# Modulation vectors of a two-layer backbone: which engine makes the first shift, and when the late vectors are made

## The chip, the cores and the metric

One core of one Trainium2 chip. The metric is the device time of one launch in microseconds (us), as the median of several runs.

## What is computed

One step of a two-layer backbone over 1024 latent tokens and 128 context tokens, width 1024, all in 32-bit floats. Each layer modulates its normalised input with vectors that depend only on the two conditions (`c` for the latent tokens, `c_ctx` for the context tokens):

```
m = silu(cond) @ w_ada + b_ada            # cond: 2 x 1024, w_ada: 1024 x 6144, per layer
sh1, sc1, g1, sh2, sc2, g2 = split(m, 6)  # parts 0 to 5, 1024 numbers each
h = rms_norm(x) * (1 + sc1) + sh1         # then layer 0: pooling + latent attention; layer 1: neighbourhood attention
x = x + g1 * mixer(h)
h = rms_norm(x) * (1 + sc2) + sh2
x = x + g2 * (square(relu(h @ w1)) @ w2)  # MLP, hidden width 4096
```

The change concerns only `m`: 2 layers x 6 parts x 2 conditions.

## The kernel before, in words

Activations lie transposed, channels on the 128 partitions, tokens along the free axis (1152 of them). Each 32-bit product is made from two rounded halves in three matmuls (`mm3`, L331). Tiles come from 36 slots of SBUF (`Slots`, L51): a new tile takes the slot that was freed longest ago. All DMAs are issued by SyncE (SP), one queue in order. The order of instructions on each engine is not the program's order: a list scheduler with a timeline of its own orders them when the kernel is built, taking on each engine the earliest program step that is ready in its timeline. What the hardware then does is in order on each engine.

A modulation vector is made in one of two ways.
- **On TensorE**, `ada_mat(part)` (L217): eight loads of 512 KB (`wadan`, each in its own slot), per load two matmuls of 512 columns with the 2-column condition as the stationary side (each appears as two instructions in the trace), then eight small transposes (`ps_at`) and the bias. Parts 0 and 1 of layer 0 are made so, one after the other, scale first, at the very start.
- **On VectorE**, `ada_gen(layer, fs)` (L192): per block `f` of 128 outputs one load of 512 KB into one of two tiles (`wada`, or a tile of the weight ring `wr` with `ring`), and two multiply-and-sum instructions (L201, `trash<-wada,silu`), one for each condition, each followed by a read of the accumulator. They need `silu`, the conditions broadcast to all partitions: two tiles of 512 KB that `silu_load` (L183) reads from a small DRAM tensor, which is stored once from a transposed copy (L520 to L524). A part is 8 blocks, 16 such instructions. After block 7 of a part, `ada_bias` finishes it.

`background(n)` (L236) takes n steps (n L201 instructions) from a list of such generators. It is called inside other loops, so that the instructions come between those of the loop.

Where the parts are made before: layer 0, parts 0 and 1 on TensorE at the start; parts 2 and 3 in the background of the input projection (L617 to L637, `NBG` = 4 steps for each tile); parts 4 and 5 by `ada_late` (L1114), run in a block after the attention of layer 0 and ahead of its output projection (`out_group`, L880). Layer 1: parts 0 and 1 in the MLP of layer 0 (`tail0(-1)`, steps in `second_tile`, L459); parts 2 to 5 in the input projection of layer 1 (L1197 to L1214, `QBG` = 2).

The attention of layer 0 (L1091 to L1110) runs head by head. `attend_units(h)` (L1057): for each of two halves nine key tiles, per tile three score matmuls (`ps_st`), an exponential on ScalarE, and the product with the values (`ps_pv`). Woven into it for heads 0 to 5 is `max_units(h+2)` (L1028), which finds the row maxima of a head two ahead: 24 matmuls (`ps_m`, three PSUM buffers) and for each a VectorE reduction (L1037). At the end of each pair of heads `recip_pair` (L1043) divides. At the start of each head the next heads' tensors are loaded, ten larger loads. TensorE runs in order, so a `ps_m` matmul whose buffer is not read yet holds all matmuls behind it.

After the attention, `split_groups` (L871, lines L876 and L877) splits the results, `out_group(0, 0, ...)` projects the first half of the tokens and adds it to `x` (L891, with gate part 2), `norm_stats` (L262) and `quad_apply` (L301, with parts 3 and 4) prepare the MLP's input and `operands` (L357) its combinations, while `out_group(0, 1, ...)` projects the second half.

Of the kernel before, what the change touches and what calls it, by code (L numbers as in the profile page):

```python
# [17 lines left out]
P = 128  # L18
# [12 lines left out]
LAG = 4  # L31
EDGE, EDGE_POOL = (0, 1), (1, 2, 4, 5, 6, 7)
XS, PSH, OW, OA, OB = (11, 11, 12, 12, 13, 13, 14, 14), (14, 14, 15, 15), 10, 8, 6
NBG = 4
QBG = 2
NEARLY = 2
GRID = 64
ROWS = NS // GRID
ROPE_THETA = 10000.0
# [51 lines left out]
def hybrid_kernel(ctx: ExitStack, tc: tile.TileContext, I, O):  # L91
# [14 lines left out]
    def PS(name, tag="pa"):  # L106
        return psum.tile([P, 512], F32, tag=tag, name=name, bufs={"pa": 3, "pb": 3, "pc": 2}[tag])
# [4 lines left out]
    def dma(out, in_):  # L112
        nc.sync.dma_start(out.bitcast(F32) if out.dtype == F32R else out,
                          in_.bitcast(F32) if in_.dtype == F32R else in_)

    def run(g):
        for _ in g:
            pass
# [64 lines left out]
    def silu_load():  # L183
        silu[:] = [S.alloc(f"silu{i}") for i in range(2)]
        for i in range(2):
            dma(silu[i][:, :D].rearrange("p (k f) -> p k f", k=KD), silu_d[:, i, :].partition_broadcast(P))
# [7 lines left out]
    def ada_gen(layer, fs, ring=False):  # L194
        rs = [] if ring else [S.alloc("wada") for _ in range(2)]
        for f in fs:
            r = W("wr", "wada") if ring else rs[f % 2]
            dma(r[:, :D], I["wada1"][f] if layer else I["wada0t"][f - 16])
            for i in range(2):
                a = ada[layer][:, f, i:i + 1]  # L200
                nc.vector.tensor_tensor_reduce(trash, r[:, :D], silu[i][:, :D], scale=1.0, scalar=0.0,  # L201
                                               op0=ALU.mult, op1=ALU.add, accum_out=a)
                yield
            if f % 8 == 7:
                ada_bias(layer, f // 8, ada[layer][:, f - 7:f + 1, :])
        S.free(*rs)
# [10 lines left out]
    def ada_mat(part):  # L217
        ps = [PS("ps_a", "pc") for _ in range(2)]
        for k in range(KD):
            r = S.alloc("wadan")  # L220
            dma(r[:, :D], I["wada0"][part, k])
            for q in range(2):
                nc.tensor.matmul(ps[q][0:2], sil[:, 2 * k:2 * k + 2], r[:, q * 512:q * 512 + 512],
                                 start=k == 0, stop=k == KD - 1)
            S.free(r)
            yield
        row = S.alloc("arow")
        for q in range(2):
            nc.scalar.copy(row[0:2, q * 512:q * 512 + 512], ps[q][0:2])
        pt = PS("ps_at", "pb")  # L230
        for k in range(KD):
            nc.tensor.transpose(pt[:, 2 * k:2 * k + 2], row[0:2, k * P:k * P + P], ident[0:2, 0:2])
        S.free(row)
        ada_bias(0, part, pt[:, 0:16].rearrange("p (k i) -> p k i", i=2))
        yield
# [3 lines left out]
    def background(n=1):  # L239
        for _ in range(n):  # L240
            while bg:
                try:
                    next(bg[0])
                    break
                except StopIteration:
                    bg.pop(0)
# [255 lines left out]
    def load_x(ch):  # L502
        for k in range(KD):
            dma(x[k][:, ch * CH:ch * CH + CH], I["xT"][k][:, ch * CH:ch * CH + CH])

    load_x(0)
    stats = [norm_stats(x, 0)]
    run(ada_mat(1))
    run(ada_mat(0))
    ws = [wtile(wsplit(I["win0"][4 + g])) for g in range(4)]  # L510
    hh, hl = alloc_h()
    norm_apply(x, hh, hl, 0, 0, 0, stats[0])
# [4 lines left out]
    dma(ecnt, I["ecnt"])  # L517
    nc.scalar.copy(sel8r, sel8)
    nc.scalar.copy(identr, ident)
    pt = PS("ps_sil", "pb")  # L520
    nc.tensor.transpose(pt[0:16, 0:P], sil, ident)
    sr = S.alloc("sr")
    nc.scalar.copy(sr[0:16, 0:P], pt[0:16, 0:P])
    dma(silu_d.rearrange("k i f -> (k i) f"), sr[0:16, 0:P])  # L524
    S.free(sr, *x)

    qd_n, qd_r = [DR(f"qdn{i}", [4, P, NS]) for i in range(2)], [DR(f"qdr{i}", [2, P, NS]) for i in range(2)]
    kd_n, kd_r = [DR(f"kdn{i}", [4, P, TOK]) for i in range(2)], [DR(f"kdr{i}", [2, P, TOK]) for i in range(2)]
# [14 lines left out]
    for ch in range(NCH):  # L543
        c0 = ch * CH
        for g in range(4):
            ps = PS("ps_i")[:, :CH]
            mm3(ps, ws[g], hs, c0, c0 + CH)
            for a, b, i in chunk_parts(ch):
# [3 lines left out]
                else:  # L552
                    nc.scalar.copy(by_block(ain[g][:, 8:8 + NS])[:, a // P:b // P],
                                   src.rearrange("p (i r c) -> p i r c", r=ROWS, c=8))

    silu_load()
    bg.append(ada_gen(0, range(16, 16 + 8 * NEARLY)))


    def window(a, b, c, g, n, e):  # L560
# [58 lines left out]
    for m in (2, 3, 0, 1):  # L619
        w = wtile(wsplit(I["win0"][m]))  # L620
        for ch in range(NCH):
            ps = PS("ps_i")[:, :CH]
            c0 = ch * CH
            mm3(ps, w, hs, c0, c0 + CH)
            if m == 3:
                nc.scalar.copy(kraw[0:64, c0:c0 + CH], ps[0:64])
            else:
                nc.scalar.copy((rq[0], rq[1], rkv)[m][:, c0:c0 + CH], ps)
            if m == 2:
                latnorm([rkv], [ckv], "kln", ch)  # L630
            if m == 1:
                if ch == 0:
                    qlat = [(S.alloc(f"qlh{i}", F32R), S.alloc(f"qll{i}", F32R)) for i in range(2)]
                latnorm(rq, qlat, "qln", ch)
            if m != 1:
                next(pg, None)
            background(NBG)  # L637
    run(pg)
    dma(O["ckv"], rkv[:, NS:])
    dma(O["krope"], kraw[0:32, NS:])  # L640
# [418 lines left out]
    def attend_units(h, qk, rest, opair, den):  # L1059
        (qh, kh), (ql, kl, vv) = qk, rest  # L1060
        v = vv.rearrange("p (t f) -> p t f", t=9)
        held = None
        for half in range(2):
            qs = slice(half * 512, half * 512 + 512)
            po = PS("ps_pv", "pc")
            for kt in range(9):
                if held is None:
                    held, n = S.alloc("p"), 0
                u = slice(512 * n, 512 * n + 512)
                ks = slice(kt * P, kt * P + P)  # L1070
                ps = PS("ps_st")
                st = nc.tensor.matmul(ps, kl[0:96, ks], qh[0:96, qs], start=True, stop=False)
                if len(mxi) >= LAG:
                    after(st, mxi[-LAG])
                nc.tensor.matmul(ps, kh[0:96, ks], ql[0:96, qs], start=False, stop=False)
                nc.tensor.matmul(ps, kh[0:97, ks], qh[0:97, qs], start=False, stop=True)
                p_ = held[:, u]
                nc.scalar.activation(p_, ps, AF.Exp, scale=scale0)
                nc.tensor.matmul(po, v[:, kt, :], p_, start=kt == 0, stop=kt == 8)  # L1079
                n += 1  # L1080
                if n == 2:
                    S.free(held)
                    held = None
                if kt == 6:
                    later()
                yield
            finish_values(64 * (h % 2), half, po, opair, den, half and h % 2)
        yield

    background(10 ** 6)  # L1090
    S.free(*silu)  # L1091
    qks = {0: load_qk(0), 1: load_qk(1)}
    weave((chain(max_units(0, qks[0]), max_units(1, qks[1])), 50), (chain(value_gen(), context_gen0()), 17),
          (mix_gen(), 13))
    rest = load_rest(0)
    opairs = []
    for h in range(8):
        if h % 2 == 0:
# [10 lines left out]
        S.free(*qks[h], *rest)  # L1109
        rest = nrest  # L1110
    later(2)
    S.free(oat)


    def ada_late():
        silu_load()
        yield from ada_gen(0, range(16 + 8 * NEARLY, 48))
        S.free(*silu)

    x = [S.alloc(f"x{k}") for k in range(KD)]  # L1120
    for k in range(KD):
        dma(x[k], I["xT"][k])
    acts = [split_groups(o) for o in pooled]
    run(ada_late())
    acts += [split_groups(o) for o in opairs]
    out_group(0, 0, [a[0] for a in acts])
    for a in acts:
# [11 lines left out]
    def tail0(ch):  # L1139
        if ch == -1:  # L1140
            silu_load()
            bg.append(chain(ada_gen(1, range(16)), free_silu()))
            return
        if ch == -2:
            for c in range(2):
                st[c] = norm_stats(x, c, HC)
            return
        if ch == 0:
            raws.append([S.alloc("nr") for _ in range(4)])
            h.extend(alloc_h())  # L1150
        if ch > 1:
            st[ch] = norm_stats(x, ch, HC)
        norm_apply(x, *h, ch, 1, 0, st[ch], HC)
# [43 lines left out]
    silu_load()  # L1197
    for g in range(4):
        if g == 1:
            bg.append(chain(ada_gen(1, range(16, 48), True), free_silu()))  # L1200
        raw, rows = raws[g % 2], slice(32 * (g % 2), 32 * (g % 2) + 8)
        pairs = (2 * g, 2 * g + 1, 2 * g, 2 * g + 1)
        order = [(t, ch) for t in range(4) for ch in range(NCH)]
# [261 lines left out]
def layout(a):  # L1465
# [11 lines left out]
    for i in range(2):  # L1477
        put(f"bada{i}", cols(a[f"b_ada_l{i}"]))
        put(f"nmix{i}", cols(a[f"norm_mix_l{i}"]))
        put(f"nmlp{i}", cols(a[f"norm_mlp_l{i}"]))  # L1480
        w = np.asarray(a[f"w_ada_l{i}"])
        if i == 0:
            r["wada0"] = np.ascontiguousarray(w[:, :2 * D].reshape(KD, P, 2, D).transpose(2, 0, 1, 3))
            r["wada0t"] = np.ascontiguousarray(w[:, 2 * D:].T).reshape(32, P, D)
        else:
            r["wada1"] = np.ascontiguousarray(w.T).reshape(48, P, D)
        r[f"w1_{i}"] = tile_w(a[f"w_mlp1_l{i}"])
        w2 = np.asarray(a[f"w_mlp2_l{i}"]).reshape(2, 8, 2, P, 4, 256)
        r[f"w2_{i}"] = np.ascontiguousarray(w2.transpose(1, 4, 3, 2, 0, 5)).reshape(8, 4, P, 1024)
# [101 lines left out]
```

## Time and profile before

| what | value |
|---|---|
| median of 3 runs | 3052.11 us (3050.89 to 3064.39) |
| the profiled execution, its own time | 3059.43 us |
| its span, first to last instruction | 3057.2 us |
| mean granted TensorE clock | 0.971 |
| busy: TensorE / VectorE / ScalarE / GpSimd | 97% / 69% / 44% / 10% |
| L201 instructions | 160: 32 in the input projection of layer 0, 32 after its attention, 32 in its MLP, 64 in the input projection of layer 1 |

Engines: PE = TensorE matmul, PEld = its weight load, DVE = VectorE, ACT = ScalarE, POOL = GpSimd, SP = SyncE. A busy PE is not PE at its peak: the ends of matmuls are modelled. Times within the span count from its first instruction.

### The profile page before, as it was taken

The page shows a single profiled execution, that of the slowest core. Times are in us where ns is not written, and L with a number is a line of the kernel's source. Part 1 is how long each engine was busy: PE and PEld are TensorE (multiplying, and loading weights), DVE is VectorE, ACT ScalarE, POOL GpSimd, SP SyncE. Part 2 cuts the span into 40 slices and gives each one's busy share as a digit, 9 for nine tenths or more (in the row PEclk, how much of TensorE's full clock was granted, in tenths as well). Part 3 has the DMA queues.
Part 4 walks back from the last instruction along what each step waited for, and adds up shares of the span by engine and source line. Part 5 has one row for each costly group of instructions (what it writes and reads, how often), then busy time and mean ns, then how long its engine had stood idle before and what let it go on. Part 6 is the DMA issues. An engine that isn't in the chain of part 4 may idle for free.

```text
span 3057.2 us, 46985 instructions
## 1 busy us (share of the span) xinstructions
PE 2950.9 (97%) x18622; PEld 2663.1 (87%) x18622; DVE 2117.4 (69%) x3777; ACT 1337.7 (44%) x2194; POOL 315.5 (10%) x210
## 2 busy tenths in 40 slices
PE   7998999889999999999999999989989999999999
PEld 4956666689999999999988797767989999999999
DVE  5976343797768889786899522544677678777775
ACT  5364344244436544353645422434345355453433
POOL 1014000252000020000221000000021000110000
PEclk9996999999999999999999999999999999999999
DMA  6529331432323334232566346687303232332322
GB/s 233 165 69 312 81 76 50 134 105 83 97 77 96 104 126 146 88 97 84 169 206 208 112 151 176 170 198 204 115 29 93 81 100 73 121 94 87 97 77 87
DMA packets 148269, 372.39 MB, mean 122 GB/s; under 512 B 14225, under 2 KB 67073, under 8 KB 148050
## 3 DMA queue, kind: packets, MB, share of 16 engines
q1 hardware_dynamic: 148050, 369.40, 39.4%
q8 instruction: 146, 2.39, 0.3%
q14 instruction: 73, 0.60, 0.1%
HBM read 310.69 MB, written 57.47 MB: 120 GB/s over the span
## 4 chain that ended last, share of the span: by engine, by line
PE 86%; DVE 5%; DMA 5%; issue 1%; ACT 1%; POOL 1%; SPq 0%; DVEq 0%; ACTq 0%; POOLq 0%
PE ps L453 9%; PE ps L455 9%; PE ps L454 9%; PE ps L423 8%; PE ps L425 7%; PE ps L424 7%; PE ps_pv L1079 4%; PE ps_pv L1336 2%; PE ps_n L336 2%; PE ps_n L337 2%; PE ps_n L338 2%; PE ps_v L1360 1%; DVE trash L201 1%; PE ps_v L1362 1%; PE ps_v L1361 1%
## 5 line engine op out<-in xcount | busy, mean ns | idle before, releaser
L453 PE MATMUL ps<-ml,wh 128*128 128x288 f32 x2048 | 591.9, 295 | 10.1 <-DVE ml L442 7.8
L454 PE MATMUL ps<-mh,wl 128*128 128x288 f32 x2048 | 600.9, 295 | 0.0
L455 PE MATMUL ps<-mh,wh 128*128 128x288 f32 x2048 | 596.5, 295 | 0.0
L423 PE MATMUL ps<-bl,wh 128*128 128x288 f32 x1792 | 532.7, 297 | 13.4 <-DVE bl L354 10.2
L424 PE MATMUL ps<-bh,wl 128*128 128x288 f32 x1792 | 529.5, 295 | 0.0
L425 PE MATMUL ps<-bh,wh 128*128 128x288 f32 x1792 | 528.0, 295 | 0.0
L453 PEld LDWEIGHTS ps<-ml,wh 128*128 128x128 f32 x2048 | 381.3, 188 | 11.1 <-DVE ml L442 8.3
L454 PEld LDWEIGHTS ps<-mh,wl 128*128 128x128 f32 x2048 | 385.2, 188 | 0.0
L455 PEld LDWEIGHTS ps<-mh,wh 128*128 128x128 f32 x2048 | 383.3, 188 | 0.1
L459 DVE SCALAR_TENSOR_TENSOR x<-ps,ada,x 128x288 f32<-128x288 f32 (+2 forms) x640 | 269.8, 450 | 120.3 <-PE ps L455 118.8
L423 PEld LDWEIGHTS ps<-bl,wh 128*128 128x128 f32 x1792 | 336.7, 188 | 16.5 <-issue 11.5
L425 PEld LDWEIGHTS ps<-bh,wh 128*128 128x128 f32 x1792 | 338.3, 189 | 0.0
L424 PEld LDWEIGHTS ps<-bh,wl 128*128 128x128 f32 x1792 | 337.4, 188 | 0.2
L396 ACT CAST wh<-s 128x512 fp32r<-128x512 f32 x256 | 146.1, 618 | 306.9 <-PE ps L455 216.6
L161 ACT CAST wh<-wr 128x1024 fp32r<-128x1024 f32 x188 | 197.0, 1049 | 169.8 <-PE ps L425 80.1
L201 DVE CUSTOM_DVE_ANT_0 trash<-wada,silu 128x1024 bf16<-128x1024 f32 x160 | 214.5, 1340 | 17.9 <-DMA wada<-in_wada 7.6
L162 DVE TENSOR_TENSOR wl<-wr,wh 128x1024 fp32r<-128x1024 f32 x144 | 179.7, 1251 | 44.9 <-ACT wh L161 44.8
L396 ACT CAST wh<-wr 128x1024 fp32r<-128x1024 f32 (+1 forms) x128 | 106.9, 835 | 219.8 <-PE ps L455 155.5
L162 POOL TENSOR_TENSOR wl<-wr,wh 128x1024 fp32r<-128x1024 f32 x44 | 124.1, 2827 | 707.2 <-ACT wh L161 707.1
L1037 DVE TENSOR_REDUCE stat<-ps_m 128x1 f32<-128x384 f32 x192 | 98.3, 551 | 121.2 <-PE ps_m L1036 120.9
L1284 DVE CUSTOM_DVE_ANT_0 trash<-ps_m,ta 128x512 bf16<-128x512 f32 (+1 forms) x128 | 84.0, 656 | 122.0 <-PE ps_m L1282 113.4
L397 DVE TENSOR_TENSOR wl<-s,wh 128x512 fp32r<-128x512 f32 x232 | 157.6, 711 | 5.1 <-ACT wh L396 2.8
(321 smaller groups left out, 6248.9 us busy)
## 6 DMA issues: line engine op xcount, KB each, us to landing
wr<-in_w SPq DMA_DIRECT2D x256, 512.0 KB
wada<-in_wada SPq DMA_DIRECT2D x48, 512.0 KB
wada<-in_wada0t SPq DMA_DIRECT2D x32, 512.0 KB
wr<-in_win SPq DMA_DIRECT2D x24, 512.0 KB
wr<-in_wout SPq DMA_DIRECT2D x24, 512.0 KB
vd<-vst SPq DMA_DIRECT2D x27, 384.0 KB
kk<-kd SPq DMA_DIRECT2D x32, 288.0 KB
nv<-vd SPq DMA_DIRECT2D x16, 576.0 KB
```

The source lines that it names most:

```text
L161: nc.scalar.copy(hi, r)
L162: (nc.gpsimd if e else nc.vector).tensor_sub(lo, r, hi)
L201: nc.vector.tensor_tensor_reduce(trash, r[:, :D], silu[i][:, :D], scale=1.0, scalar=0.0, op0=ALU.mult, op1=ALU.add, accum_out=a)
L396: nc.scalar.copy(h, src)
L397: (nc.gpsimd if j in EDGE and min(ps) in EDGE_POOL else nc.vector).tensor_sub(l, src, h)
L423: nc.tensor.matmul(ps, wh[:, a], hl[:, b], start=k == 0, stop=False)
L424: nc.tensor.matmul(ps, wl[:, a], hh[:, b], start=False, stop=False)
L425: nc.tensor.matmul(ps, wh[:, a], hh[:, b], start=False, stop=k == 3)
L453: nc.tensor.matmul(ps, wh, hl, start=kk == 0, stop=False)
L454: nc.tensor.matmul(ps, wl, hh, start=False, stop=False)
L455: nc.tensor.matmul(ps, wh, hh, start=False, stop=kk == 3)
L459: nc.vector.scalar_tensor_tensor(x[m][:, a:b], ps[:, a - ch * HC:b - ch * HC], g, x[m][:, a:b], op0=ALU.mult, op1=ALU.add)
```

## The change

The first shift (part 0 of layer 0) is made on VectorE, woven with the scale on TensorE; for that `silu` is stored and loaded at the start. The input projection of layer 0 has no background any more. Parts 2 to 5 of layer 0 and parts 0 and 1 of layer 1 (96 steps) are made in the background of the attention of layer 0, one step in two of three key tiles. `ada_late` is gone. The MLP of layer 0 makes parts 2 and 3 of layer 1, the input projection of layer 1 parts 4 and 5. The weights' layout in DRAM follows.

```diff
-            dma(r[:, :D], I["wada1"][f] if layer else I["wada0t"][f - 16])
+            dma(r[:, :D], I["wada1"][f] if layer else I["wada0t"][f if f < 8 else f - 8])
...
+    pt = PS("ps_sil", "pb")
+    nc.tensor.transpose(pt[0:16, 0:P], sil, ident)
+    sr = S.alloc("sr")
+    nc.scalar.copy(sr[0:16, 0:P], pt[0:16, 0:P])
+    dma(silu_d.rearrange("k i f -> (k i) f"), sr[0:16, 0:P])
+    silu_load()
     load_x(0)
     stats = [norm_stats(x, 0)]
-    run(ada_mat(1))
-    run(ada_mat(0))
+    weave((ada_mat(1), 9), (ada_gen(0, range(8)), 16))
+    S.free(sr, *silu)
     ws = [wtile(wsplit(I["win0"][4 + g])) for g in range(4)]
...
-    silu_load()
-    bg.append(ada_gen(0, range(16, 16 + 8 * NEARLY)))
...
-            background(NBG)          # in the input projection of layer 0
...
                 if kt == 6:
                     later()
+                if kt % 3:
+                    background()     # in attend_units
                 yield
...
     rest = load_rest(0)
+    silu_load()
+    bg.append(chain(ada_gen(0, range(16, 48)), ada_gen(1, range(16)), free_silu()))
...
     later(2)
+    background(10 ** 6)
...
-    run(ada_late())
...
-            bg.append(chain(ada_gen(1, range(16)), free_silu()))            # tail0
+            bg.append(chain(ada_gen(1, range(16, 32)), free_silu()))
...
-            bg.append(chain(ada_gen(1, range(16, 48), True), free_silu()))  # layer 1
+            bg.append(chain(ada_gen(1, range(32, 48), True), free_silu()))
```

## Rows read from the trace of the kernel before

**Rows 1.** The first part of the page: busy time of each engine over the span, its share, and the number of instructions.

```profile
PE 2950.9 (97%) x18622; PEld 2663.1 (87%) x18622; DVE 2117.4 (69%) x3777; ACT 1337.7 (44%) x2194; POOL 315.5 (10%) x210
```

**Rows 2.** Busy time by stretches of the span. Columns: the stretch, its length, then busy time and instructions of PE, PEld, DVE, ACT and POOL, the granted TensorE clock, the DMA engines' busy share, and GB/s. 12 to 47.6: the scale and the shift on TensorE. 79 to 156: input projection of layer 0 with 32 L201 instructions. 220 to 310: start of the attention. 310 to 510: heads 0 to 5. 510 to 568.6: heads 6 and 7. 568.6 to 700: `ada_late` and the output projection, up to the first matmul of the MLP. 1100 to 1240: MLP of layer 0 with 32 L201 instructions. 1545 to 1665: input projection of layer 1 with 49 of them. 2300 to 3057: a stretch without any.

```profile
0.00:12.00 12.00, 0.03 (x1) 0.06 (x2) 3.57 (x8) 5.89 (x11) 3.34 (x7) 1.00 0.79 249
12.00:47.60 35.60, 33.18 (x84) 7.23 (x84) 14.54 (x24) 13.52 (x25) 6.97 (x5) 0.99 0.99 379
...
79.00:156.00 77.00, 77.00 (x434) 75.00 (x432) 73.01 (x148) 27.94 (x56) 0.00 (x0) 1.00 0.53 160
...
220.00:290.00 70.00, 56.80 (x193) 42.07 (x191) 52.84 (x98) 31.87 (x41) 40.77 (x25) 0.66 0.83 307
290.00:310.00 20.00, 15.01 (x52) 10.09 (x52) 12.90 (x32) 6.81 (x23) 2.34 (x1) 0.74 1.07 258
310.00:510.00 200.00, 200.00 (x699) 131.00 (x699) 84.76 (x161) 77.52 (x132) 4.77 (x2) 0.97 0.26 62
510.00:568.60 58.60, 58.60 (x206) 36.67 (x205) 18.86 (x31) 24.56 (x41) 2.37 (x1) 1.00 0.34 108
568.60:700.00 131.40, 107.94 (x753) 106.62 (x752) 121.81 (x165) 41.69 (x66) 58.44 (x24) 0.90 0.35 113
...
1100.00:1240.00 140.00, 134.78 (x1005) 133.37 (x1004) 134.60 (x246) 59.99 (x76) 5.95 (x2) 1.00 0.47 150
1545.00:1665.00 120.00, 120.00 (x628) 103.59 (x627) 117.68 (x193) 53.42 (x98) 23.72 (x8) 1.00 0.57 188
2300.00:3057.00 757.00, 751.63 (x5645) 750.13 (x5643) 553.02 (x962) 337.98 (x453) 36.39 (x22) 1.00 0.30 92
```

**Rows 3.** Waits of TensorE between 560 and 740 us: who waited for what, us in total, times, the longest.

```profile
PE ps_o L336 <- DVE oa L877: 10.9, 1, 10.9
PE ps_n L275 <- DVE nt L273: 8.9, 1, 8.9
PE ps_o L336 <- DVE x L891: 3.7, 2, 3.2
```

**Rows 4.** Groups of VectorE instructions between 568.6 and 650 us: busy us, mean ns of one, and idle time before them with what ended it.

```profile
L201 DVE CUSTOM_DVE_ANT_0 trash<-wada,silu 128x1024 bf16<-128x1024 f32 x32 | 50.4, 1575 | 3.6 <-DMA wada<-in_wada0t 3.2
...
L211 DVE TENSOR_TENSOR ada<-ada,vec 128x16 f32<-128x16 f32 x2 | 3.8, 1913 | 0.0
```

**Rows 5.** The end of the attention in order of time, lines of GpSimd, VectorE and TensorE: start, length, engine, line, operation, count, and in brackets the idle time before it.

```profile
573.41 2.40 POOL L1047 TENSOR_TENSOR den<-den,ry 128x1024 f32<-128x1024 f32 x1 [56.24 <-ACT ry L1046]
...
581.41 1.22 DVE L1048 SCALAR_TENSOR_TENSOR den<-den,ry 128x1024 f32<-128x1024 f32 x1
...
583.69 1.22 DVE L1049 SCALAR_TENSOR_TENSOR o<-o,den 128x1024 f32<-128x1024 f32 x1
584.83 0.45 DVE L876 CAST oa<-o 128x576 fp32r<-128x576 f32 x1
...
588.89 1.42 DVE L877 TENSOR_TENSOR oa<-o,oa 128x576 fp32r<-128x576 f32 x2
...
578.54 0.29 PE L338 MATMUL ps_o<-oa,wh 128*128 128x288 f32 x1
589.70 0.61 PE L336 MATMUL ps_o<-oa,wh 128*128 128x288 f32 x1 [10.86 <-DVE oa L877]
```

**Rows 6.** Busy time by stretches of 10 us behind that wait, columns as in rows 2.

```profile
590.00:600.00 10.00, 10.00 (x66) 10.00 (x66) 9.97 (x17) 2.95 (x6) 2.40 (x1) 0.84 0.50 157
600.00:610.00 10.00, 10.00 (x78) 10.00 (x77) 9.71 (x14) 2.33 (x3) 6.64 (x3) 1.00 0.59 162
```

**Rows 7.** All L201 instructions of the run: duration in ns (least, median, most), start of the first and of the last, and their form.

```profile
L201 DVE CUSTOM_DVE_ANT_0 trash<-wada,silu x160: 1203/1218/3384, 79.1 to 1665.8; 128x1024 bf16<-128x1024 f32 x160
L201 DVE DVE_READ_ACCUMULATOR2_ANT ada<- x160: 70/81/89, 80.3 to 1666.9; 128x1 f32 x160
```

**Rows 8.** The loads at the start of a head (SP's queue, first and last line of ten loads; start, length of the issue).

```profile
345.38 0.45 SPq L113 DMA_DIRECT2D kh<-kdn  x1
...
350.84 0.58 SPq L113 DMA_DIRECT2D ql<-qdr  x1
```

**Rows 9.** The first 50 us in order of time, lines of SP, TensorE, ScalarE and VectorE; columns as in rows 5.

```profile
5.92 15.20 SPq L113 DMA_DIRECT2D wadan<-in_wada  x16
22.08 2.89 SPq L113 DMA_DIRECT2D wr<-in_win  x3
25.92 13.54 SPq L113 DMA_DIRECT2D x<-in_xT  x16
...
16.74 12.18 PE L223 MATMUL ps_a<-wadan,sil 128*2 128x512 f32 x28
32.32 1.04 ACT L161 CAST wh<-wr 128x1024 fp32r<-128x1024 f32 x1 [2.79 <-DMA wr<-in_win]
45.09 0.16 DVE L211 TENSOR_TENSOR ada<-ps_at,vec 128x16 f32<-128x16 f32 x1
47.66 0.69 PE L336 MATMUL ps_i<-hl,wh 128*128 128x384 f32 x1
```

**Rows 10.** Pieces of the chain that ended last: start, length, what. The first lies at the start of the attention, the second in `ada_late`, the last at the start of layer 1.

```profile
297.87 7.65 DMA kh<-kdr
...
599.20 3.70 DMA wada<-in_wada0t
...
1511.94 6.00 DMA silu<-silud
```

More of the change, by code (lines that the diff above doesn't have):

```diff
@@ L33 @@
 XS, PSH, OW, OA, OB = (11, 11, 12, 12, 13, 13, 14, 14), (14, 14, 15, 15), 10, 8, 6
-NBG = 4
 QBG = 2
-NEARLY = 2
 GRID = 64
@@ L220, in ada_mat @@
             r = S.alloc("wadan")
-            dma(r[:, :D], I["wada0"][part, k])
+            dma(r[:, :D], I["wada0"][k])
             for q in range(2):
@@ L519, in hybrid_kernel @@
     nc.scalar.copy(identr, ident)
[L520 to L525, printed above, removed]
+    S.free(*x)
     qd_n, qd_r = [DR(f"qdn{i}", [4, P, NS]) for i in range(2)], [DR(f"qdr{i}", [2, P, NS]) for i in range(2)]
@@ L1088, in attend_units @@
         yield
-    background(10 ** 6)
-    S.free(*silu)
     qks = {0: load_qk(0), 1: load_qk(1)}
@@ L1111, in hybrid_kernel @@
     later(2)
+    background(10 ** 6)
     S.free(oat)
[L1115 to L1118, printed above, removed]
     x = [S.alloc(f"x{k}") for k in range(KD)]
@@ L1482, in layout @@
         if i == 0:
-            r["wada0"] = np.ascontiguousarray(w[:, :2 * D].reshape(KD, P, 2, D).transpose(2, 0, 1, 3))
-            r["wada0t"] = np.ascontiguousarray(w[:, 2 * D:].T).reshape(32, P, D)
+            r["wada0"] = np.ascontiguousarray(w[:, D:2 * D]).reshape(KD, P, D)
+            r["wada0t"] = np.ascontiguousarray(np.concatenate([w[:, :D], w[:, 2 * D:]], axis=1).T).reshape(40, P, D)
         else:
```

## The prediction

> **What bounds the kernel now.** I read the busy shares first: TensorE works 97% of the span [rows 1], so time can be won only where it stands, or by taking work from it. The table by stretches shows where it stands [rows 2]. The input projection of layer 0 (79 to 156) has it busy 77.0 of 77 us although VectorE, with 32 multiply-and-sum instructions, is busy 73.0; the input projection of layer 1 (1545 to 1665) 120 of 120, with 49 of them; the attention 200 of 200 and 58.6 of 58.6. The stretch from the end of the attention to the first MLP matmul (568.6 to 700) has it busy 107.9 of 131.4: 23.5 us lost, at a mean clock of 0.90. The list of its waits puts all of that on VectorE: 10.9 us on the split of the last heads' output, 8.9 us on the norm's sums, 3.7 us on residual adds [rows 3]. And VectorE is there full of `ada_late`: 50.4 us of multiply-and-sum, at 1575 ns each instead of the usual 1218, and 3.8 us of biases [rows 4, 7].
>
> The first 47.66 us are the other place: TensorE makes both vectors in one run and the first real matmul waits for the shift (bias at 45.09, matmul at 47.66) [rows 9]. The DMA engines are busy 0.99 at 379 GB/s there [rows 2].
>
> **The change, part by part.**
>
> *The stretch behind the attention* loses 32 instructions. At 578.83 TensorE has used up the matmuls that don't need the last heads; it goes on at 589.70 [rows 5]. GpSimd ended its multiplication at 575.81. What must follow on VectorE is two products of 1.22 us, one cast of 0.45 and one subtraction of 0.7: 3.6 us, so 579.4; the rest is the instructions that go. 10.2 us are won. Behind that wait the clock was down: 66 matmuls in 10 us instead of 78 [rows 6], 12 x 0.13 = 1.6 us. Of the 8.9 us on the norm's sums the ordinary latency of the chain (one square, two adds) stays, an estimate of 2 us, so 7 are won. The 3.7 us come from the MLP's operands on VectorE, which stay. 10.2 + 1.6 + 7 = 18.8; with a little of the clock behind the second wait I take **-20**. Bounds: -10 (the first wait alone) to -27 (23.5 + 1.6, and a second clock dip of the same order).
>
> *The attention* gains 96 instructions, each 1.22 + 0.08 us [rows 7]. Heads 0 to 5 lie in 310 to 510, VectorE busy 84.8 of 200; 72 new ones make 93.6, together 178: 89%. Heads 6 and 7: 18.9 + 24 x 1.3 = 50 of 58.6 [rows 2]. So it fits, but the cover is thin, and it is no longer true that VectorE only waits: a multiply-and-sum whose load is late holds the row-maximum reductions behind it, these hold the three PSUM buffers, and TensorE in order then holds the scores and values. If the cover is gone every us of VectorE is one of TensorE. No row has this exact mix. Nearest from above: the MLP of layer 0 with 32 such instructions, VectorE at 134.6 of 140, lost 5.2 us of TensorE, where a stretch without any loses 5.4 in 757 or 1.0 in 140: 4.2 us for 32, 12.6 for 96. From below: the input projection of layer 1, VectorE 117.7 of 120, lost nothing [rows 2]. A gain is excluded, TensorE being full. In the MLP VectorE frees PSUM, as here, but it is fuller than 89%; I take half: **+6**, bounds 0 to +13.
>
> *Its loads.* 48 loads of 512 KB join SP's queue in the attention, which moves 62 GB/s in heads 0 to 5 [rows 2]; 36 of them there are 18.9 MB in 200 us, 94 GB/s more, far below the 379 seen. But at each head ten loads are issued in a row over 6 us [rows 8], and the next `wada` stands behind them: that is the last rival. The two `silu` loads (1 MB) come where the attention starts, and there the chain that ended last runs through `kh<-kdr` [rows 10] with the DMA engines at 1.07 and 307 to 258 GB/s [rows 2]; 1.05 MB at 379 is 2.8 us. **+2**, bounds 0 to +6 (the 6.0 us that the same load took at the start of layer 1 [rows 10]).
>
> *The start.* TensorE loses half of its vector work: 32 instructions at 0.435 us (28 in 12.18 [rows 9]), 13.9 us. VectorE gets 16 at 1.3: 20.8 us in a stretch of 35.6 where it is busy 14.5 [rows 2], so it fits narrowly. What decides is when its data come. `silu` must be transposed, stored, and loaded back, behind the first loads: vectors and `x` 1.8 MB, some four weight loads 2.1, itself 1.05, some 4.9 MB; 3.0 are moved by 12 us (249 GB/s), the rest at 379 by 17 (all an estimate from rows 2). From there VectorE alone would need 20.8 us to 37.8, plus the 2.57 from bias to first matmul and 0.6 of the end: 41.0, a gain of 6.7. But the blocks pass through two tiles: block f+2 is loaded only after block f is read. How long does a load take? In `ada_late` 3.7 us [rows 10], in this stretch 10.2, from the issue of the first weight of the input projection at 22.08 to its cast at 32.32 [rows 9], because the queue is deep. Block 0 is read by 19.6; three more rounds of load + 2.6 us follow, then block 7 with 2.6 and the 3.2 us of the end: with 3.7 us loads 19.6 + 18.9 + 5.8 = 44.3 (-3.4), with 10.2 us ones 63.8 (+16). The early loads meet the deep queue, the later ones an emptying one (the loads of `x` are issued by 39.5 [rows 9]), and the scheduler may put the blocks ahead of these. I take **+5**, between the ends; bounds -7 to +16. The work behind, with TensorE full in 79 to 156 [rows 2], passes any delay on.
>
> *Others.* The input projection of layer 0 loses 32 instructions and 16 loads, that of layer 1 half of its own: TensorE is full in both, 0 (a gain excluded by that, a loss by there being less to do). The MLP of layer 0 makes other parts at the same cost: 0.
>
> Sum: -20 + 6 + 2 + 5 = -7. The profiled execution took 3059.4 us in all (span 3057.2); -7 makes 3052.4. It stands 7.3 us above the median of the runs, 3052.1, so on the median I predict **3045**.
>
> **The rivals.**
>
> *Only TensorE's own work counts.* The 13.9 us taken from TensorE at the start come through in full, and what moves between stretches of VectorE is worth nothing, because behind the attention something else (the weights' splits on GpSimd, the loads of `x`) is as late as `ada_late` was: 3052.1 - 13.9 = 3038. For it: TensorE is busy 97% [rows 1]. Against: the waits of [rows 3] are all on VectorE and as long together as 23.5 us. Chance 0.06. The Trainium skill ("Perfetto Trace Analysis", section Identifying Performance Opportunities) says that kernels improve by improving the performance of the most-contended engine; by that rule the time would be the 3038 of this rival, and the trace agrees with it for the kernel as a whole, not for the stretch behind the attention.
>
> *Both covers hold.* The attention loses nothing, as the projection of layer 1 did; the first shift runs at VectorE's own pace (-6.7); the stretch behind the attention gains 23.5 + 1.6 = 25. With +2 for `silu`: -30, 3022. For it: VectorE at 89% is below both compared stretches. Against: two tiles and a 10 us load at the start. Chance 0.28.
>
> *The shift is not beside the scale but behind it.* Each round of two tiles waits 10 us; the first matmul starts at 63.8: -20 + 6 + 2 + 16 = +4, 3056. For it: the 10.2 us load. Against: the queue empties. Chance 0.10.
>
> *VectorE becomes the attention's bound (slower).* At each of heads 0 to 5 the next block stands behind ten loads: 6 us of issue [rows 8]; VectorE stands that long with the reductions behind it, and with 11% of slack (3.5 of some 33 us a head) and three PSUM buffers already behind, it does not catch up: 6 x 6 = 36 us. -20 + 36 + 2 + 5 = +23, 3075. It decides from about 3.5 us of lost VectorE time a head. For it: `ada_late` itself ran at the pace of its loads at several places. Against: VectorE waited for such loads 3.2 us in all behind the attention [rows 4], and the scheduler can put reductions ahead. Chance 0.12.
>
> **How the numbers follow.** The forecast has 0.44; its own range, from the sizes of its four terms, is 3034 to 3056. 0.5% is 15.3 us, about what a measurement of this kernel can tell from no change: faster below 3036.8, slower above 3067.4. Faster: 0.28 and a tenth of the forecast, 0.32. Slower: the last rival, 0.12. The rest, 0.56, is within. The range reaches to the rival in which both covers hold and most of the way to the last: 3022 to 3062.
>
> **What would show it.** Right: the wait of `ps_o` on the split falls from 10.9 to under 2 us and that of `ps_n` from 8.9 to about 2; the first MLP matmul comes some 20 us sooner after the last value product; VectorE near 89% in heads 0 to 5, a few us of new TensorE waits on L1037 there; the first `ps_i` matmul near 52 us. Wrong: waits of `ps_m` on VectorE of over 15 us (last rival), a first matmul near 41 or past 60, or waits behind the attention that stay as they are (first rival).

## The result, and the profile after

The changed kernel takes **3067.79 us** (median of 11 runs, 3060.43 to 3073.55), the kernel before 3052.11 beside it (11 runs, 3041.23 to 3064.39). The ratio is 1.0048, with a 95% interval of 1.0032 to 1.0064: slower by 0.5%, where 3045 was forecast and 3022 to 3062 was the range. The profiled execution after took 3062.2 us (span 3060.4), against 3059.4 before.

Lines after are lower by two (L201 is now L199, L336 is L334), in the attention by five (L1037 is now L1032, L1079 is L1074).

First the engines' busy time of the kernel after, the answer to [rows 1]:

```profile
PE 2921.7 (95%) x18582; PEld 2644.2 (86%) x18582; DVE 2133.0 (70%) x3809; ACT 1338.6 (44%) x2192; POOL 302.4 (10%) x210
```

TensorE is busy 29 us less, yet the kernel is slower. Half of that is work taken away: 40 instructions fewer (18622 to 18582), the 32 products and 8 transposes of the shift, 14.8 us by their busy time before. The rest is the same instructions with shorter mean durations. So TensorE has less to do and stands more. Where, is seen in the stretches, answering to [rows 2] with the same columns, one line for each: the first 12 us, the next 35.6, on to the first `ps_i` matmul, the start of the attention (first row-maximum matmul to first value product), the attention (to the last value product), and behind it to the first MLP matmul.

```profile
0.00:12.00 12.00, 0.37 (x1) 0.09 (x1) 2.85 (x7) 5.59 (x11) 2.19 (x6) 1.00 0.63 184
12.00:47.60 35.60, 17.94 (x42) 3.78 (x42) 20.93 (x32) 11.21 (x21) 4.87 (x6) 0.90 1.00 373
47.60:73.50 25.90, 1.66 (x3) 0.51 (x3) 23.48 (x39) 7.92 (x16) 4.52 (x3) 0.50 0.34 102
280.40:354.00 73.60, 53.75 (x182) 38.88 (x183) 59.53 (x99) 24.54 (x52) 16.41 (x15) 0.69 0.92 297
354.00:608.50 254.50, 250.46 (x866) 158.97 (x865) 200.26 (x363) 99.05 (x169) 7.56 (x3) 1.00 0.52 153
608.50:712.80 104.30, 100.39 (x750) 99.47 (x749) 71.53 (x98) 41.86 (x65) 48.74 (x23) 1.00 0.22 66
```

The stretch behind the attention is what the change was forecast to make of it: TensorE stands 3.9 us in place of 23.5, at a clock of 1.00 in place of 0.90. The third row is new: 25.9 us in which TensorE runs three matmuls. TensorE's waits in the first 720 us, the answer to [rows 3] and more:

```profile
PE ps_i L334 <- DVE hl L293: 21.0, 1, 21.0
PE ps_m L1031 <- DVE stat L1032: 17.0, 10, 8.8
PE ps_a L221 <- DMA wadan<-in_wada: 13.8, 1, 13.8
PE ps_n L273 <- DVE nt L271: 13.7, 1, 13.7
...
PE ps_o L334 <- DVE oa L872: 2.6, 1, 2.6
...
PE ps_o L334 <- DVE x L886: 1.3, 1, 1.3
```

The waits behind the attention went (10.9 to 2.6, 8.9 to nothing, 3.7 to 1.3); the 13.8 on `wadan` and the 13.7 on `nt` end at 18.3 and 50.8 us, at the start. Two larger ones came: 21.0 us for the first input of the projection, and 17.0 on the row maxima, one of them 8.8 us long. Waits of over 15 us on the row maxima were to be the sign of the rival in which VectorE bounds the attention; but between the first and the last value product they are only 3.0 us:

```profile
PE ps_m L1031 <- DVE stat L1032: 3.0, 4, 1.4
```

The others stand ahead of that, at the start of the attention.

The wait of 21.0 us, in order of time: the loads on SP from 13 us on, then VectorE's multiply-and-sums around the gap, then TensorE's first projection matmul (the answer to [rows 9]).

```profile
13.10 5.49 SPq L111 DMA_DIRECT2D wadan<-in_wada  x7
19.54 2.89 SPq L111 DMA_DIRECT2D wr<-in_win  x3
23.38 4.17 SPq L111 DMA_DIRECT2D x<-in_xT  x4
28.55 0.33 SPq L111 DMA_DIRECT2D wada<-in_wada0t  x1
29.78 3.46 SPq L111 DMA_DIRECT2D x<-in_xT  x4
33.47 0.33 SPq L111 DMA_DIRECT2D wada<-in_wada0t  x1
...
47.09 3.56 SPq L111 DMA_DIRECT2D wada<-in_wada0t  x2
...
56.49 5.20 SPq L111 DMA_DIRECT2D wada<-in_wada0t  x2
```

```profile
18.91 1.21 DVE L199 CUSTOM_DVE_ANT_0 trash<-wada,silu 128x1024 bf16<-128x1024 f32 x1
...
21.43 1.22 DVE L199 CUSTOM_DVE_ANT_0 trash<-wada,silu 128x1024 bf16<-128x1024 f32 x1
...
37.77 6.01 DVE L288 SCALAR_TENSOR_TENSOR ht<-x,ada,nt 128x384 f32<-128x384 f32 x7
43.70 1.21 DVE L199 CUSTOM_DVE_ANT_0 trash<-wada,silu 128x1024 bf16<-128x1024 f32 x1
...
67.27 1.22 DVE L199 CUSTOM_DVE_ANT_0 trash<-wada,silu 128x1024 bf16<-128x1024 f32 x1
...
69.68 0.96 DVE L209 TENSOR_TENSOR ada<-ada,vec 128x16 f32<-128x16 f32 x1
...
73.49 0.69 PE L334 MATMUL ps_i<-hl,wh 128*128 128x384 f32 x1 [21.03 <-DVE hl L293]
```

Block 0 is read by 20.1 us, block 1 by 22.6. The load of block 2 into the first tile goes out at 28.55, behind weights and `x`, that of block 3 at 33.47; and in VectorE's order block 2 is read only behind the scale's use on `x` (L288): for 21 us, from 22.6 to 43.7, no block is read. The last two loads go out from 56.49 on. The shift is complete at 70.6, TensorE starts at 73.49 in place of 47.66.

From block 4 on SP is no longer late: each load goes out within 0.1 us of the reading of its tile (47.09 for 47.05, 61.37 for 61.33). And VectorE hardly waits for blocks: between 12 and 73.5 us twice, 5.6 us for the first block and 1.2 for the last. On the chain that ended last, between 38.30 and the first matmul, a block's load stands only once, the last one, 3.56 us; the rest is mostly VectorE, whose order puts norm sums and `ht` lines of further columns between the products. The wait in total, then the piece of the chain:

```profile
DVE trash L199 <- DMA wada<-in_wada0t: 6.8, 2, 5.6
...
61.37 3.56 DMA wada<-in_wada0t
```

The 8.8 us, lines of VectorE, GpSimd and TensorE:

```profile
282.06 9.08 DVE L823 TENSOR_TENSOR pl<-pooled,ph 128x1152 fp32r<-128x1152 f32 x1
...
292.46 1.34 DVE L823 TENSOR_TENSOR pl<-pooled,ph 128x1152 fp32r<-128x1152 f32 x1
...
281.96 2.34 POOL L688 TENSOR_TENSOR tq<-tq,fh 128x1024 fp32r<-128x1024 f32 x1
...
284.77 2.60 POOL L688 TENSOR_TENSOR tk<-tk,fh 128x1152 fp32r<-128x1152 f32 x1
...
287.59 2.33 POOL L688 TENSOR_TENSOR tq<-tq,fh 128x1024 fp32r<-128x1024 f32 x1
...
291.67 1.62 PE L1031 MATMUL ps_m<-kh,qh 96*128 96x384 f32 x3 [8.78 <-DVE stat L1032]
```

The same subtraction takes 1.34 us and, the first time, 9.08. It starts 0.10 us after a GpSimd subtraction and ends 1.2 us after the third of them (289.92), about its own length. Behind it stand the row maxima, behind these TensorE. No multiply-and-sum has run there yet.

### The profile page after: what moved, and what is told of

The parts are those of the page before. It is cut to its first block, busy times and chain, and to the rows that moved or that the text cites. A ratio compares the mean times of both kernels' runs of the same rounds, so it can differ in the third digit from the quotient of the medians.

```text
span 3060.4 us, 46941 instructions
## 1 busy us (share of the span) xinstructions
PE 2921.7 (95%) x18582; PEld 2644.2 (86%) x18582; DVE 2133.0 (70%) x3809; ACT 1338.6 (44%) x2192; POOL 302.4 (10%) x210
## 4 chain that ended last, share of the span: by engine, by line
PE 83%; DVE 7%; DMA 6%; issue 2%; ACT 2%; SPq 1%; POOL 0%; DVEq 0%; ACTq 0%
PE ps L451 9%; PE ps L453 9%; PE ps L452 9%; PE ps L421 8%; PE ps L423 7%; PE ps L422 7%; PE ps_pv L1074 3%; PE ps_pv L1328 2%; PE ps_n L334 2%; PE ps_n L335 2%; PE ps_n L336 2%; DVE trash L199 2%; PE ps_o L334 1%; PE ps_o L335 1%; PE ps_o L336 1%
## 5 line engine op out<-in xcount | busy, mean ns | idle before, releaser
L421 PE MATMUL ps<-bl,wh 128*128 128x288 f32 x1792 | 532.8, 298 | 13.2 <-DVE bl L352 10.2
L199 DVE CUSTOM_DVE_ANT_0 trash<-wada,silu 128x1024 bf16<-128x1024 f32 x176 | 221.3, 1257 | 28.0 <-DMA wada<-in_wada0t 14.3
L160 POOL TENSOR_TENSOR wl<-wr,wh 128x1024 fp32r<-128x1024 f32 x44 | 115.7, 2636 | 873.1 <-ACT wh L159 826.7
L1074 PE MATMUL ps_pv<-p,v 128*128 128x512 f32 x288 | 146.3, 592 | 0.0
```

Source lines behind the costliest of these rows:

```text
L160: (nc.gpsimd if e else nc.vector).tensor_sub(lo, r, hi)
L421: nc.tensor.matmul(ps, wh[:, a], hl[:, b], start=k == 0, stop=False)
```

## The experiments

In this table all times are us from the traces, but for the last columns: first projection matmul (`ps_i`); from there to the first row-maximum matmul; on to the first value product; to the last one; to the first MLP matmul; when that comes; then the median of the runs and the ratio to the kernel before in the same series. Behind the first MLP matmul the kernels do the same work (but for 32 multiply-and-sums more in layer 1's input projection in the kernel before and in only_start), and one stretch of that, layer 1's attention, lasted 306 to 328 us in the profiled executions; so effects are read from the stretches and from the ratios, not from single spans. Each kernel was profiled once, so how far a stretch varies between executions of one kernel is not measured; where the edits leave a stretch alone it differs little (first `ps_i` 47.5 to 48.3 in the six kernels with eight tiles and VectorE's splits, 104.2 to 105.8 behind the attention in the nine with the late vectors in it and two tiles for them).

| kernel | first ps_i | projection | start of attention | attention | behind it | first MLP | median | ratio |
|---|---|---|---|---|---|---|---|---|
| before | 47.7 | 209.0 | 62.5 | 248.8 | 131.0 | 699.0 | 3052.1 | 1 |
| after | 73.5 | 206.9 | 73.6 | 254.5 | 104.3 | 712.8 | 3067.8 | 1.0048 |
| undo_start | 48.4 | 208.0 | 72.0 | 257.5 | 104.4 | 690.3 | 3047.3 | 0.9976 |
| only_start | 72.2 | 212.9 | 59.7 | 248.7 | 126.0 | 719.5 | 3073.6 | 1.0071 |
| two_first | 63.1 | 210.5 | 68.7 | 258.8 | 104.3 | 705.4 | 3064.5 | 1.0035 |
| four_tiles | 62.7 | 207.1 | 69.4 | 254.9 | 104.2 | 698.3 | 3052.2 | 0.9994 |
| eight_tiles | 47.7 | 209.2 | 65.1 | 257.2 | 105.8 | 685.0 | 3038.3 | 0.9947 |
| silu_keep | 69.5 | 212.1 | 64.6 | 256.3 | 105.8 | 708.3 | 3061.1 | 1.0016 |
| e8_keep | 47.9 | 223.0 | 64.7 | 259.4 | 105.8 | 700.8 | 3053.0 | 1.0007 |
| e8_plpool | 47.5 | 210.1 | 57.9 | 257.6 | 105.7 | 678.8 | 3038.2 | 0.9952 |
| e8_loadonly | 48.0 | 209.3 | 66.0 | 269.9 | 105.5 | 698.7 | 3049.1 | 0.9995 |
| e8_att4 | 48.3 | 209.1 | 67.2 | 248.6 | 109.7 | 682.9 | 3035.2 | 0.9943 |
| e8_att4_plpool | 47.5 | 211.5 | 63.0 | 251.0 | 109.5 | 682.5 | 3036.6 | 0.9944 |
| e8_att4_wl | 50.0 | 210.7 | 69.0 | 249.4 | 108.5 | 687.6 | 3039.9 | 0.9958 |

**The halves of the change.** undo_start:

```
-    weave((ada_mat(1), 9), (ada_gen(0, range(8)), 16))
+    run(ada_mat(1))
+    run(ada_mat(0))        # the silu store behind load_x again, as before; the rest as after
```

> The changed kernel with the start put back: both first vectors on TensorE, the shift's store and the silu load where they were; the move of the late vectors into the attention stays. Theory A (the start makes the loss: two tiles and their place in SP's queue): the first input projection matmul is back near 47.7 us, some 25 us earlier than in the changed kernel, and the time is 3067.8 - 25 = about 3042, that is 10 below the kernel before. Rival B (the loss is made in the attention, and what the start loses would be made good behind it anyway): the time stays within 5 us of the changed kernel, 3063 to 3068.

only_start is the kernel before with the opposite edit.

> The kernel before with only the first shift put on VectorE; the late vectors stay where they were. Theory A: first input projection matmul near 73 us, time 3052 + 25 = 3077, slower than the whole change. Rival B: no more than 5 us over the kernel before, 3052 to 3057.

Measured: 0.9976 (0.9957 to 0.9995) and 1.0071 (1.0044 to 1.0098); their product, 1.0047, is the whole change's 1.0048. So the halves add up: moving the late vectors gains some 7 us, the start loses some 22. Theory A holds, rival B falls. The times are 5 and 3 us off what theory A gave (3042 and 3077), which is within the intervals.

**Why the start loses.** eight_tiles gives every block its own tile (`ada_gen(0, range(8), nt=8)`, `rs[f % nt]`):

```
-        rs = [] if ring else [S.alloc("wada") for _ in range(2)]
+        rs = [] if ring else [S.alloc("wada") for _ in range(nt)]
```

> The changed kernel with eight tiles for the eight blocks of the shift in place of two, so that no load waits for a block to be read; the same bytes, the same 16 multiply-and-sums. Theory A: blocks 2 to 7 are loaded between the weights of the scale, the first input projection matmul comes at 41 to 50 us and the time is 24 to 32 below the changed kernel, 3036 to 3044. Rival C (the start is limited by the bytes or by VectorE's own work, not by the two tiles): first matmul at 65 us or later, time 3060 or more.

First matmul at 47.7, ratio 0.9947 (0.9929 to 0.9965), below undo_start and below the kernel before. What it has over undo_start is not won here (47.7 against 48.4), but mostly in the start of the attention (65.1 against 72.0). The same bytes and the same 16 products: rival C falls. Of its trace, the last load of a block, the end of the products on VectorE, the first matmul, and the stretch around them:

```profile
25.59 0.33 SPq L111 DMA_DIRECT2D wada<-in_wada0t  x1
...
37.26 1.22 DVE L199 CUSTOM_DVE_ANT_0 trash<-wada,silu 128x1024 bf16<-128x1024 f32 x1
...
40.94 4.32 DVE L288 SCALAR_TENSOR_TENSOR ht<-x,ada,nt 128x384 f32<-128x384 f32 x8
...
47.72 0.69 PE L334 MATMUL ps_i<-hl,wh 128*128 128x384 f32 x1 [10.19 <-DVE hl L293]
...
20.00:40.00 20.00, 15.59 (x40) 2.89 (x38) 19.65 (x36) 5.09 (x8) 0.00 (x0) 1.00 1.03 407
```

All eight loads are out at 25.59 in place of 61.37, and VectorE is busy 19.65 of 20 us. It is now what ends last, so that even here nothing is won at the start over the kernel before: the products end at 38.5, and the splits and `ht` lines that stand behind them on VectorE take 9.2 us more, so that the first matmul comes as late as with the shift on TensorE.

two_first keeps two tiles and puts the loads of `x` behind them:

```
+            if ch:
+                after(d, wl_[0])     # in load_x: d follows the last wada load on SP
```

> The changed kernel, still with two tiles for the shift, but the 16 loads of the later columns of x are made to follow the last block of the shift in SP's queue. It parts the two halves of theory A. Theory A1 (the place in the queue: blocks 2 and 3 were issued at 28.55 and 33.47 us, behind weights and x): first input projection matmul at 46 to 55 us, time 18 to 27 below the changed kernel, 3041 to 3050. Theory A2 (two tiles alone: each round of load and read is paid whatever stands beside it): first matmul at 62 us or later, time within 10 of the changed kernel, 3057 to 3067.

63.1 us: with `x` behind the blocks 10.4 of the 25.8 us go, and 15.4 stay with the two tiles. That is theory A2 by its own bound, though with a good part of A1 in it. (The edit also moved four weight loads and VectorE's order, so the split is rough.) The first MLP matmul comes 7.4 us earlier; the time, 1.0035 (1.0017 to 1.0053), isn't apart from that of the change.

four_tiles is eight_tiles with `nt=4`.

> The changed kernel with four tiles for the shift at the start: one reuse of every tile in place of three, while blocks 4 to 7 still stand behind the loads of x in SP's queue. If each reuse costs the start its own share (25.8 us for three, none for none), the first input projection matmul comes at 54 to 60 us and the time is 14 to 20 below the changed kernel, 3048 to 3054. If the place in the queue is all that counts, whatever the number of reuses, it comes at 65 us or later and the time is 3058 or more.

62.7 us and 0.9994 (0.9982 to 1.0005): the time fell as expected, in part by luck: the matmul did not come at 54 to 60, and 4.2 of the 14.5 us at the first MLP matmul come from the start of the attention. The cost isn't a fixed share for each reuse: in its trace blocks 4 to 7, the only ones that need a free tile, go out between the loads of `x` from 28.87 on, and VectorE reads them from 42.77 to 56.5, behind the scale's eight `ht` instructions, without a wait for a block. One reuse is enough to put a block behind all of that.

**The attention.** e8_loadonly shortens the instructions:

```
-                nc.vector.tensor_tensor_reduce(trash, r[:, :D], silu[i][:, :D], ...
+                nc.vector.tensor_tensor_reduce(trash[:, :n], r[:, :n], silu[i][:, :n], ...   # n=16 in the attention
```

> The kernel with eight tiles; the 96 multiply-and-sums inside the attention of layer 0 take 16 columns in place of 1024 (the late vectors are left out of the computation so), the 48 loads stay. It tells which of the two costs the attention its 6 to 9 us. Theory H (VectorE's time): from the first to the last value product 248 to 251 us as in the kernel before (eight tiles 257), time 6 to 10 below eight tiles. Rival I (the loads in SP's queue and on the DMA engines): 255 us or more, time within 3 of eight tiles.

VectorE's time in the attention fell from 205 to 111 us, and the attention became 12.7 us longer, 0.9995 (0.9977 to 1.0013) in all. So it isn't VectorE's time. Its waits for the blocks in that stretch:

```profile
DVE trash L199 <- DMA wada<-in_wada0t: 49.5, 28, 4.9
...
DVE trash L199 <- DMA wada<-in_wada: 19.8, 14, 2.4
```

69.3 us, where eight_tiles waits 11.4 (below): the in-order VectorE stands on a load with the row maxima behind it. Shorter instructions also let the scheduler order them otherwise; that this made the waits longer is argued, not shown. Rival I is closer, but its numbers were exceeded; the edit changed the order as well as the work.

e8_att4 gives those blocks four tiles (`nt=4` in the two generators).

> The kernel with eight tiles at the start (3038 us), and four tiles in place of two for the blocks inside the attention, so that a load can be issued two blocks ahead. With two tiles SP's queue stood 99 us in that stretch for a block to be read, VectorE 11 us for blocks to land, and from the first to the last value product it took 257 us, 8 more than in the kernel before. Theory I (late loads, held up by the two tiles, hold VectorE and the row maxima behind it): SP's wait falls under 30 us, the stretch comes to 248 to 252 us, time 5 to 9 below eight tiles, 3029 to 3033. Rival H (VectorE's own time: 96 more instructions in it): the stretch stays at 255 us or more, 3036 to 3041.

The attention takes 248.6 us, as in the kernel before. The attention in eight_tiles and in e8_att4 (columns as in [rows 2]), then VectorE's waits for blocks in the one and in the other, then SP's for a block to be read:

```profile
322.00:579.20 257.20, 250.94 (x872) 159.60 (x870) 205.28 (x373) 99.80 (x169) 7.55 (x3) 1.00 0.52 155
```

```profile
324.60:573.20 248.60, 247.90 (x863) 159.12 (x862) 200.44 (x366) 99.55 (x169) 7.15 (x3) 1.00 0.53 158
```

```profile
DVE trash L199 <- DMA wada<-in_wada0t: 8.4, 6, 3.6
...
DVE trash L199 <- DMA wada<-in_wada: 3.0, 4, 1.5
...
SPq L111 <- DVE ada L199: 99.0, 36, 4.3
```

```profile
DVE trash L199 <- DMA wada<-in_wada: 1.2, 1, 1.2
...
SPq L111 <- DVE ada L199: 78.7, 31, 4.3
```

The same 200 us of VectorE, at 39 of 40 us in the fullest slices, cost TensorE nothing once the blocks are there in time. The two other kernels with four tiles there agree (251.0 and 249.4), while all with two and the 96 full multiply-and-sums lie at 254.5 to 259.4. Theory I holds for the stretch, though here too the edit can have changed the scheduler's order; that SP would stand under 30 us was wrong (78.7), it stands with the load two blocks further ahead. The stretch behind became 3.9 us longer, so the first MLP matmul came only 2.1 earlier and the ratio, 0.9943 (0.9920 to 0.9965), isn't apart from that of eight_tiles.

**The start of the attention.** silu_keep removes the two `silu` loads in front of it:

```
-    S.free(sr, *silu)
+    S.free(sr)
...
-    silu_load()          # in front of head 0
```

> The changed kernel with the two silu tiles kept from the start, so that the two 512 KB loads in front of the attention go. It asks what makes the 11 us that the start of the attention lost. Theory D (the silu loads ahead of the first heads' tiles in SP's queue): first value product 6 to 11 us earlier against the last pooled projection, time 6 to 11 below the changed kernel, 3057 to 3062. Rival E (the multiply-and-sums stand on VectorE in front of the row maxima of heads 2 and 3): less than 3 us, 3065 to 3068.

e8_keep is the same on eight_tiles.

> The kernel with eight tiles (3038 us), and the silu tiles kept from the start, so that the two loads in front of the attention go. Theory D (these loads are late in the way of the first heads): 3 to 8 below eight tiles, 3030 to 3035. Rival E (with eight tiles the loads were issued at 292 us, early enough): 3036 to 3041.

The first gained 9 us at the start of the attention and lost 5.2 in the projection, the time fell to 1.0016 (0.9997 to 1.0036), within theory D's numbers; the second gained 0.4 there, lost 13.8 in the projection (a new wait of 6.3 us of `ps_i` on ScalarE's `ain` is part of that) and all of eight_tiles' gain: 1.0007 (0.9992 to 1.0023). Two slots fewer give later tiles other slots, which is argued as the cause, not shown. And in silu_keep the split of the pooled vectors on VectorE (`pl`, L823, the 9.08 us above) started later beside GpSimd and took 3.2 us instead of 9.1, 5.9 us less; in e8_keep it took 3.1. So the loads weren't shown to cost anything; with eight tiles theory D's gain did not come.

e8_plpool moves that subtraction:

```
-            nc.vector.tensor_sub(pl, mx, ph)
+            nc.gpsimd.tensor_sub(pl, mx, ph)
```

> The kernel with eight tiles, and the four splits of the pooled vectors (pl) on GpSimd instead of VectorE. In the changed kernel and with eight tiles one of these subtractions lasted 9.1 us instead of 1.35 on VectorE, just while GpSimd ran its own subtractions back to back, and ended with them; TensorE stood 8.8 us behind it at the start of the attention. Theory F (VectorE's instruction was held for as long as GpSimd ran): on GpSimd it takes some 2.6 us in its place in GpSimd's own queue, the 8.8 us wait falls under 4, time 3 to 9 below eight tiles, 3029 to 3035. Rival G (the subtraction waited for its data, and TensorE with it): the wait stays at 7 or more, 3036 to 3041.

The four subtractions take 2.6 us each on GpSimd, TensorE's wait of 8.8 us is gone (1.8 in all on the row maxima there), and the start of the attention falls from 65.1 to 57.9 us, less than before the change, with the `silu` loads in it. Theory F holds for the stretch. The time, 0.9952 (0.9931 to 0.9973), 3038.2 us, missed theory F's range and doesn't show the 7 us; the interval is wider than that.

e8_att4_plpool joins both.

> The same with the four splits of the pooled vectors on GpSimd too: the version that takes all three causes away. If each holds by itself: start as in eight tiles (first input projection matmul near 47.7), first row-maximum product to first value product near 58 us, value products 248 to 252 us, time 3023 to 3031. If the attention is VectorE's own time: value products 255 us or more, 3030 to 3039.

0.9944 (0.9927 to 0.9962), 3036.6 us, above what was expected: the start of the attention took 63.0 in place of 58, 4.2 less than without that edit, with a new wait of 4.0 us on the values' load. Causes found one by one did not add up here.

e8_att4_wl tests theory F from the other side: `wsplit(I["win0"][4 + g], 1)`, the projection's first splits on GpSimd.

> The kernel with eight tiles at the start and four in the attention (3035 us), and the first four weight splits (wl) of the input projection on GpSimd instead of VectorE. With eight tiles VectorE works without a gap from 18 to 47.7 us, the first matmul, and three of its instructions there are such splits, 3.6 us. If VectorE's own work sets the start, the first matmul comes at 43 to 45 us, time 3030 to 3033. Theory F again, from the other side: a subtraction on GpSimd, some 2.3 us each, holds VectorE's instructions with two SBUF inputs, so that some multiply-and-sums beside it last over 1.5 us in place of 1.22, and the first matmul stays at 46 to 50, time 3034 to 3038.

Lines of VectorE and GpSimd:

```profile
38.67 2.19 DVE L209 TENSOR_TENSOR ada<-ada,vec 128x16 f32<-128x16 f32 x1
...
40.99 8.38 DVE L288 SCALAR_TENSOR_TENSOR ht<-x,ada,nt 128x384 f32<-128x384 f32 x8
...
38.26 4.89 POOL L160 TENSOR_TENSOR wl<-wr,wh 128x1024 fp32r<-128x1024 f32 x2 [21.10 <-ACT wh L159]
```

A bias on 16 columns takes 2.19 us in place of 0.17, the eight `ht` 8.38 in place of 4.32 (two of the eight take 2.6 and 2.7 us), and the first matmul comes at 50.0, later than with VectorE's own splits (48.3). The ratio is 0.9958 (0.9942 to 0.9973). All but the end of the last product was over when GpSimd began, so the products stayed at 1.22, which theory F had otherwise; its 46 to 50 us for the first matmul hold, and the time is 2 us above its range.

The best version is eight_tiles, with or without four tiles in the attention: 0.5 to 0.6% below the kernel before, 1% below the change.

## Why the prediction was wrong

By the profile the first MLP matmul came 13.8 us later than before; the terms were to bring it 7 earlier.

- **The start: +5 forecast (-7 to +16), +25.8 measured.** This step failed, and alone it turns the sign. The rotation of two tiles was named as what decides, and worked out as rounds of a load and 2.6 us of reading. Two things were taken as nothing. The first is the time from a tile's being read to the issue of its next load: it was 8 and 11 us for the first two, because SP is in order and 3 weights and 4 to 8 pieces of `x` were put ahead. The second is VectorE's order: blocks 2 and 3 were read 15 and 14 us after the issue of their loads, behind the scale's work on `x` and without a wait of VectorE for them, and the later products stand between norm work of further columns, with 1.2 us of waiting for a block. "The scheduler may put the blocks ahead of these" was the hope, and +16 was no bound, since it left both out. That two_first's 63.1 us lies near the rival's 63.8 is luck: the rival took loads of 10.2 us, on two_first's chain they take 3.6 and 3.9. The lower bound failed too: with the blocks there in time the products ended at 38.5 as estimated (37.8), but 9.2 us, not 3.2, stand between them and the first matmul, so nothing was to be won (eight_tiles, 47.7).
- **The `silu` loads at the start of the attention: +2 (0 to +6), the stretch +11.1.** The loads were not shown to matter. 7 us of such a stretch in eight_tiles, 4 in e8_att4, are one subtraction held beside GpSimd, which the term did not know. It comes with the move of the late vectors: undo_start has it (8.9 us), only_start doesn't (1.8); that the stretch's instructions were laid out in another order once the multiply-and-sums had left the projection is the likely reason, not a tested one. Why the stretch takes 73.6 us in the changed kernel and 65.1 with eight tiles stays open; the loads are issued 39 and 36 us behind its start.
- **The attention: +6 (0 to +13), +5.7 measured.** The size is right by luck. It was taken from the MLP, where VectorE is nearly full; but it is late loads through two tiles, which the term named and did not price, and with four tiles it is nothing. That is the mechanism of the slower rival, at a sixth of its price.
- **Behind the attention: -20 (-27 to -10), -26.7 measured.** Right in kind, at its best bound: the wait on the norm's sums went wholly, and the clock stayed at 1.00.
- **The rest: 0 forecast; -2.1 in the projection.** Within what orders do to it (206.9 to 212.9 in kernels with the same slots for it).

Sum: 25.8 - 2.1 + 11.1 + 5.7 - 26.7 = 13.8, and the medians differ by 15.7. How near these two lie is in part chance: the two profiled executions differ by only 3.2 us in span, since behind the first MLP matmul the one after took 10.6 us less, and over all kernels here that rest lies between 2344 and 2369 us. The rival with the nearest cause ("not beside the scale but behind it", 3056) was given 0.10, and its price was still 12 us short. The rival by which TensorE's own work is all that counts is refuted: 14.8 us less of it, 0.5% slower.

## What to carry to other kernels

A rotation of two tiles is priced by when the next load can be *issued*, not by how long a load takes: count what stands ahead of it in the in-order queue, and what the reading engine's order puts before the reading. Where slots are free, as in the first 50 us here, give each block its own tile: it changed a loss of 0.5% into a gain of 0.5%. Before calling an engine too full, look whether it waits for data: VectorE at 39 of 40 us, with the data there, cost TensorE nothing.

## What was not expected of the hardware

VectorE's instruction with two operands in SBUF waits while GpSimd subtracts: 9.08 us in place of 1.34 across three GpSimd subtractions with memsets between. Other cases waited for a single one. In e8_att4_wl the bias of 2.19 us ended at 40.87, the first GpSimd subtraction at 40.84. The kernel before had it already in the slow biases of [rows 4], one of which ended 0.03 us after one GpSimd subtraction:

```profile
606.38 1.92 DVE L211 TENSOR_TENSOR ada<-ada,vec 128x16 f32<-128x16 f32 x1
...
604.89 3.36 POOL L162 TENSOR_TENSOR wl<-wr,wh 128x1024 fp32r<-128x1024 f32 x1
```

Instructions with one operand in PSUM show no such thing beside the same run of GpSimd (`tk<-tk,vec,ps_b`, three in 1.72 us). The Trainium skill ("SBUF — State Buffer", sections Who interferes with whom and SBUF: two separate sides) says that a VectorE instruction with two SBUF inputs contends with a GpSimd instruction that reads SBUF, and that the one that starts first has the ports for the whole instruction while the other is blocked. The biases agree with both. The subtraction agrees with the first part; had it been held by the one GpSimd instruction that was running when it started, it would have waited 2.2 us (to 284.30), not the 7.7 that it did. Why it did not get in between the three stays open.
